# One core, a fp32 decoder trunk: the low parts of the weights at another place in a 256-byte line

## The chip, the core and the metric

The kernel runs on one core of a Trainium2 chip. The metric is the device time of one execution in microseconds (us). Before the change the median of three runs is 2539.53 us (2539.25 to 2539.55).

Five engines run side by side, each through its own queue in order: PE multiplies matrices (its weight loads, PEld, overlap its matmuls), ACT and DVE work element by element, POOL and SP here mostly start DMA transfers. SBUF is the memory on the core, 128 partitions wide; PSUM takes the sums of the matmuls. A matmul has a *stationary* operand, which a weight load brings into the array first, and a *moving* one, whose columns then stream through it.

## The reference

Two layers at sequence length 256 and width 2048, fp32 in and out: a Mamba-2 layer and an attention layer, each followed by a gated MLP with a short convolution (inner width 5632), each with a residual LayerNorm.

```python
def conv_ffn(x, w_up, conv_w, conv_b, w_down):
    u = causal_dwconv(x @ w_up, conv_w, conv_b)
    gate, val = u[..., :D_FF], u[..., D_FF:]
    return (jax.nn.silu(gate) * val) @ w_down
...
    for layer in range(DEPTH):
        if layer < N_A_LAYERS:
            mix = mamba2_mixer(h, mamba_w_in[layer], mamba_conv_w[layer], mamba_conv_b[layer],
                               mamba_dt_bias[layer], mamba_a_log[layer], mamba_d[layer],
                               mamba_norm_w[layer], mamba_w_out[layer])
        else:
            j = layer - N_A_LAYERS
            mix = moba_cross_attention(h, attn_w_q[j], attn_w_o[j], k_blk, v_blk, k_mean)
        h = layer_norm(DEEPNORM_ALPHA * h + mix, ln_mix_g[layer], ln_mix_b[layer])
        ffn = conv_ffn(h, ffn_w_up[layer], ffn_conv_w[layer], ffn_conv_b[layer], ffn_w_down[layer])
        h = layer_norm(DEEPNORM_ALPHA * h + ffn, ln_ffn_g[layer], ln_ffn_b[layer])
        if layer == N_A_LAYERS - 1:
            k_blk, v_blk, k_mean = shared_kv(h, w_kv)
```

Nearly all of the work is the products with weights: `mamba_w_in`, `mamba_w_out`, `ffn_w_up`, `ffn_w_down`, `w_kv`, `attn_w_q` and `attn_w_o`.

## The kernel before

Each fp32 number is split into a high part, rounded to float32r, and a low part, the rest. A product is the sum of three: high x high, high x low and low x high.

The weights come in 880 tiles of 512 KB (128 partitions x 1024 elements), one per *step*. `load` (L171 to L179) brings a tile into `raw` (4 buffers); `split` (L181 to L202) makes `hi` from it on ScalarE (L200) and `lo` on VectorE (L201), into four buffers each of the pool `wts`. For the few steps in `spare` the two go into free parts of the activations' buffer `hT` instead. Loads, splits and matmuls are issued in an order written out by hand: `products` (L299) issues a step's matmuls, with the splits of later steps in their midst; `at`, `beyond` and the like hang all other work on steps.

There are two ways to multiply.

- Mode "W" (the first products of a layer, for example `ffn_w_up`): the weights are stationary, 128 columns at a time, and the activations move. `some` (L241) issues, for a step, eight matmuls with `hi` stationary (L256) past which the activation's high and low parts stream together (512 columns), and eight with `lo` stationary (L259) past which the high part streams alone (256 columns). `whole` (L273) orders them in runs of one kind: 16 of `hi`, then 16 of `lo`, or 32 and 32 where two steps are paired.
- Mode "X" (the products back, for example `ffn_w_down`): the activations are stationary and the weights move, 512 columns at a time; `half` (L212) issues L222 (`hi` past the activation's high part), L223 (`lo` past the same) and L227 (`hi` past the low part). In the last steps of a chunk the pieces are 256 columns.

One small chunk (mode "H", L270) has both parts stationary.

**Places.** Call a tile's start address modulo 256 bytes its place in a line. `LINE` is 64 elements, 256 bytes. Before, all that a product with weights reads has one and the same place: `hi`, `lo`, `raw`, the activations `hT`, `yT`, `gT` and `aT`, and, as slices are 512, 1024 or 2048 bytes apart, every slice of these that is loaded or streamed. The scratch tile `u` lies 32 bytes off that place, `sz` on it.

In the Mamba layer, a group of heads uses two more tiles of 2048 bytes: `xe` (tag "xe", written at L780, read by the matmul of L803) and `sq` (tag "sq", written at L831 and L832, read by the matmul of L838), one buffer each.

Of the kernel before, what the change touches and what calls it, by code (L numbers as in the profile page):

```python
# [19 lines left out]
F32R = mybir.dt.float32r  # L20
# [4 lines left out]
P = 128  # L25
D = 2048
S = 256
# [12 lines left out]
NC = 512  # L40
HC = NC // 2
NEG = -1.0e30
LINE = 64
# [16 lines left out]
def chunks():  # L60

    z, b, c, dt = 0, 2 * DI, 2 * DI + NG * DS, 2 * DI + 2 * NG * DS

    def some(mode, name, layer, c0, n, nk):
        return [(mode, name, layer, c0 + i * NC, nk, False) for i in range(n)]

    def ffn(layer):
        up = [some(m, "ffn_w_up", layer, c + j * NC, 1, KD)[0] for j in range(DFF // NC)
              for m, c in (("W" if j else "X", 0), ("W", DFF))]
        return up + some("X", "ffn_w_down", layer, 0, 4, KF)  # L70

    out = some("W", "mamba_w_in", 0, b, 2, KD)
    out[0] = out[0][:5] + (True,)
    out += some("H", "mamba_w_in", 0, dt, 1, KD) + some("W", "mamba_w_in", 0, c, 2, KD)
    for g in range(NG):
        out += some("W", "mamba_w_in", 0, DI + g * NC, 1, KD) + some("W", "mamba_w_in", 0, z + g * NC, 1, KD)
    out += some("X", "mamba_w_out", 0, 0, 4, DI // P) + ffn(0)
    out += some("X", "w_kv", None, D, 1, KD) + some("W", "w_kv", None, 0, 4, KD) + some("W", "attn_w_q", 0, 0, 4, KD)
    return out + some("X", "w_kv", None, D + NC, 3, KD) + some("X", "attn_w_o", 0, 0, 4, KD) + ffn(1)
# [12 lines left out]
def yoco_kernel(ctx: ExitStack, tc: tile.TileContext, x, lmg, lmb, lfg, lfb, x_t, columns, w, out):  # L92
    nc = tc.nc
    base = ctx.enter_context(tc.tile_pool(name="base", bufs=1))
    wts = ctx.enter_context(tc.tile_pool(name="wts", bufs=LA + 1))
# [30 lines left out]
    steps, plan = [], chunks()  # L126
# [44 lines left out]
    def load():  # L171
        i = pos["load"]
        if i >= n_steps:
            return
        pos["load"] += 1
        t = wts.tile([P, 2, NC], F32, tag="raw", name="raw", bufs=RAW)
        for e in (slice(0, 1), slice(1, 2)) if i == 0 else (slice(0, 2),):
            nc.sync.dma_start(t[:, e], w[i][:, e])
        raw_t[i] = t  # L179

    def split():  # L181
        i = pos["split"]
        pos["split"] += 1
        t = raw_t.pop(i)
        if i in spare:
            h, l = (bufs["h"][:, k:k + 2].rearrange("p k a t -> p k (a t)") for k in (spare[i], spare[i] + 2))
        else:
            h = wts.tile([P, 2, NC], F32R, tag="hi", name="hi")
            l = wts.tile([P, 2, NC], F32R, tag="lo", name="lo")
        hi_t[i], lo_t[i] = h, l  # L190
        if steps[i][0].mode == "H":
            for a, w in enumerate((h, l)):
                v = t[:, a].rearrange("p (k n) -> p k n", k=8)
                w = w.rearrange("p a (k e n) -> p (a k) e n", e=2, n=NC // 8)
                nc.scalar.copy(w[:, :, 0], v)
                nc.vector.tensor_sub(w[:, :, 1], v, w[:, :, 0].bitcast(F32))
            return load()
        for e in ((0,), (1,)) if i < 2 else ((0, 1),):
            sl = slice(e[0], e[-1] + 1)
            nc.scalar.copy(h[:, sl], t[:, sl])  # L200
            nc.vector.tensor_sub(l[:, sl], t[:, sl], h[:, sl].bitcast(F32))  # L201
        load()  # L202

    def splits(i, most=2):

        for _ in range(1 if steps[i][0] in calm else most):
            j = pos["split"]
            ahead = LA + 1 + sum(i <= k < j for k in spare)
            if j < min(i + ahead, n_steps) and (j in spare or sum(k not in spare for k in hi_t) < LA + 1):
                split()  # L210
# [151 lines left out]
    bufs = {"h": base.tile([P, KD, 2, S], F32R, name="hT")}  # L362
# [179 lines left out]
    def open_pool(name):  # L542
        g = tc.tile_pool(name=name, bufs=1)
        pool[name] = (g, g.__enter__())
        return pool[name][1]
# [26 lines left out]
    calm.append(chB[0])  # L572
    put_x(0)
    split()
    put_x(2)
    split()
    for p in range(2, 8):
        amid(p - 2, put_x, 2 * p)


    mp = open_pool("mamba")
# [123 lines left out]
    G = [dict() for _ in range(NG)]  # L705
# [121 lines left out]
        nc.vector.tensor_add(sz[:, 0], sz[:, 0], sz[:, 1])  # L827

    def z_cut(g):
        G[g]["sq"] = q = mp.tile([P, 2, S], F32R, tag="sq", name="sq", bufs=1)  # L830
        nc.scalar.copy(q[:, 0], G[g]["sz"][:, 0])  # L831
        nc.vector.tensor_sub(q[:, 1], G[g]["sz"][:, 0], q[:, 0].bitcast(F32))  # L832

# [40 lines left out]
    for g in range(NG):  # L874
# [22 lines left out]
        at(s0 + 20, z_square, g)  # L897
        at(s0 + 21, z_sum, g)
        at(s0 + 22, z_cut, g)
        at(s0 + 23, z_rms, g)  # L900
        at(s0 + 24, z_log, g)
# [217 lines left out]
    for h in range(HEADS):  # L1119
        i, j = divmod(h, 4)  # L1120
# [87 lines left out]
```

## Time and profile before

| | |
|---|---|
| median of 3 runs | 2539.53 us |
| the profiled execution | 2539.57 us |
| its span, first to last instruction | 2537.3 us |
| granted clock of PE | 0.999 |
| weight tiles moved | 880, 512 KB each |

A row of a group has line, engine, operation, what it writes and reads, shapes, count, then the busy time in us, the mean duration of one in ns, and the idle time before it. A matmul's duration runs from its start to the modelled end of its pipeline, so the durations of a run overlap; a row of the timeline that merges n of them is n - 1 spacings and one duration long. The chain of waits counts for each matmul only the time until the next.

### The profile page before, as it was taken

The numbers are of one execution on the slowest core, as the hardware profiler recorded it, in microseconds if no ns is written. First come the engines' busy times: TensorE is split into PE (matmuls) and PEld (weight loads), VectorE is DVE, ScalarE is ACT, GpSimd is POOL, SyncE is SP. The second block draws the span as 40 slices with busy tenths as digits, with TensorE's granted clock in tenths as the row PEclk, the third lists the DMA queues.
The fourth block names the chain that finished last, engine by engine and source line by source line (L and its number), as shares of the span: only waits on it lengthen the run. The fifth ranks groups of instructions, "written<-read, shape, count | busy, mean of one in ns | idle before, by whom it ended". The sixth has DMA issues, their size and how long they took to land.

```text
span 2537.3 us, 36085 instructions
## 1 busy us (share of the span) xinstructions
PE 2524.6 (100%) x13983; PEld 2197.0 (87%) x13983; DVE 1657.9 (65%) x2140; ACT 1365.5 (54%) x1790; POOL 76.6 (3%) x96
## 2 busy tenths in 40 slices
PE   9999999999999999999999999999999999999998
PEld 8888888888888888888888888888888888888887
DVE  7778778755666766666445646645767676765545
ACT  6677787643465555554334445543555555554333
POOL 0000000000200000000000200000200000000001
PEclk9999999999999999999999999999999999999999
DMA  7666665666665555556676655456655555566664
GB/s 253 202 194 199 205 194 186 196 208 223 213 202 189 190 188 189 191 183 200 204 235 203 209 194 168 159 180 227 221 187 193 191 187 190 183 199 200 199 227 163
DMA packets 141739, 502.59 MB, mean 198 GB/s; under 512 B 15856, under 2 KB 16368, under 8 KB 141568
## 3 DMA queue, kind: packets, MB, share of 16 engines
q1 hardware_dynamic: 136448, 482.92, 58.2%
q0 software_dynamic: 4832, 16.85, 2.1%
q8 instruction: 109, 1.79, 0.3%
q14 instruction: 62, 0.51, 0.1%
q10 hardware_dynamic: 288, 0.52, 0.1%
HBM read 491.77 MB, written 8.45 MB: 197 GB/s over the span
## 4 chain that ended last, share of the span: by engine, by line
PE 99%; DMA 0%; DVE 0%; SPq 0%; issue 0%; ACT 0%
PE acc L256 40%; PE acc L259 21%; PE acc L222 11%; PE acc L223 11%; PE acc L227 11%; PE acc L794 1%; PE tp L396 0%; PE tp L227 0%; PE tp L223 0%; PE tp L222 0%; DMA raw<-in_w 0%; PE tp L803 0%; PE acc L777 0%; PE tp L1073 0%; PE tp L1107 0%; PE tp L1099 0%
## 5 line engine op out<-in xcount | busy, mean ns | idle before, releaser
L201 DVE TENSOR_TENSOR lo<-raw,hi 128x1024 fp32r<-128x1024 f32 (+1 forms) x869 | 1059.9, 1225 | 749.6 <-ACT hi L200 616.6
L200 ACT CAST hi<-raw 128x1024 fp32r<-128x1024 f32 (+1 forms) x869 | 908.6, 1048 | 857.8 <-PE acc L227 371.9
L256 PE MATMUL acc<-hT,hi 128*128 128x512 f32 x4480 | 1059.4, 391 | 1.1 <-ACT hi L200 1.1
L256 PEld LDWEIGHTS acc<-hT,hi 128*128 128x128 f32 x4480 | 828.4, 188 | 166.0 <-ACT hi L200 2.0
L259 PEld LDWEIGHTS acc<-hT,lo 128*128 128x128 f32 x4480 | 562.8, 191 | 15.8 <-issue 1.2
L259 PE MATMUL acc<-hT,lo 128*128 128x256 f32 x4480 | 570.6, 283 | 0.0
L223 PE MATMUL acc<-lo,gT 128*128 128x512 f32 (+1 forms) x678 | 254.5, 378 | 0.0
L222 PE MATMUL acc<-hi,gT 128*128 128x512 f32 (+1 forms) x678 | 254.1, 377 | 0.0
L227 PE MATMUL acc<-hi,gT 128*128 128x512 f32 (+1 forms) x678 | 200.7, 377 | 0.0
L222 PEld LDWEIGHTS acc<-hi,gT 128*128 128x128 f32 x678 | 127.6, 188 | 23.2
L223 PEld LDWEIGHTS acc<-lo,gT 128*128 128x128 f32 x678 | 127.6, 188 | 23.1
L227 PEld LDWEIGHTS acc<-hi,gT 128*128 128x128 f32 x678 | 124.8, 188 | 23.8
L223 PE MATMUL acc<-lo,yT 128*128 128x512 f32 (+1 forms) x270 | 98.6, 369 | 0.0
L222 PE MATMUL acc<-hi,yT 128*128 128x512 f32 (+1 forms) x270 | 98.5, 369 | 0.0
L222 PE MATMUL acc<-hi,hT 128*128 128x512 f32 x192 | 78.8, 410 | 0.0
L227 PE MATMUL acc<-hi,yT 128*128 128x512 f32 (+1 forms) x270 | 77.7, 369 | 0.0
L223 PE MATMUL acc<-lo,hT 128*128 128x512 f32 x192 | 75.4, 393 | 0.0
L599 DVE TENSOR_TENSOR u<-u,acc 128x512 f32<-128x512 f32 x108 | 73.4, 681 | 2.3 <-ACT u L598 1.4
L626 DVE SCALAR_TENSOR_TENSOR g<-u,cols,g 128x254 f32<-128x254 f32 (+1 forms) x176 | 73.3, 478 | 0.7 <-ACT g L621 0.7
L626 DVE SCALAR_TENSOR_TENSOR v<-u,cols,v 128x254 f32<-128x254 f32 (+1 forms) x176 | 73.0, 477 | 0.0
L1023 ACT CAST gT<-v 128x512 fp32r<-128x512 f32 x44 | 27.3, 621 | 84.5 <-DVE v L1022 84.5
L458 POOL TENSOR_TENSOR rs<-rs,mhalf 128x1 f32<-128x1 f32 x8 | 7.5, 932 | 2002.2 <-DVE nb L459 2002.2
(223 smaller groups left out, 1911.3 us busy)
## 6 DMA issues: line engine op xcount, KB each, us to landing
raw<-in_w SPq DMA_DIRECT2D x880, 512.0 KB, 3.6
mA<-acum_d POOLq DMA_DIRECT2D x16, 512.0 KB, 6.4
hres<-r POOLq DMA_DIRECT2D x12, 512.0 KB, 6.7
r<-hres SPq DMA_DIRECT2D x12, 512.0 KB, 4.9
eA<-acum_d POOLq DMA_DIRECT2D x16, 128.0 KB, 7.5
r<-in_x SPq DMA_DIRECT2D x4, 512.0 KB, 5.1
gb<-in_ln_mix_g SPq DMA_DIRECT2D x8, 256.0 KB, 4.8
gb<-in_ln_mix_b SPq DMA_DIRECT2D x8, 256.0 KB, 5.0
```

The lines of the kernel that those rows point to most:

```text
L200: nc.scalar.copy(h[:, sl], t[:, sl])
L201: nc.vector.tensor_sub(l[:, sl], t[:, sl], h[:, sl].bitcast(F32))
L222: nc.tensor.matmul(a, th, h[:, kk, sl], start=k == 0, stop=False)
L223: nc.tensor.matmul(a, th, l[:, kk, sl], start=False, stop=False)
L227: nc.tensor.matmul(a, ch.x.lo(k)[:, ts], h[:, kk, sl], start=False, stop=k == ch.nk - 1)
L256: nc.tensor.matmul(banks[j], w[:, kk, js], ch.x.both(k), start=begins, stop=ends, skip_group_check=True)
L259: nc.tensor.matmul(banks[j][:, :S], w[:, kk, js], ch.x.hi(k), start=begins, stop=ends, skip_group_check=True)
L458: nc.gpsimd.tensor_tensor(self.rs[:, h, :], self.rs[:, h, :], mhalf[:, 0, :], op=OP.pow)
L599: nc.vector.tensor_add(dst, dst, p[:, :, :S])
L626: nc.vector.scalar_tensor_tensor(d, u[:, i % 2, :S - k], c1(self.at_w, w[n - 1 - k] + self.ia + i), d, op0=OP.mult, op1=OP.add)
L794: nc.tensor.matmul(ps[64 * q:64 * q + 64, c, j * P:(j + 1) * P], G[g]["xdt"][:, c, h * 64:(h + 1) * 64], G[g]["A", c][:, h, :], start=True ...
L1023: nc.scalar.copy(h, v[:, sl])
```

## The change

In mode "W", `lo` starts 192 bytes (three quarters of a line) into its buffer; elsewhere it starts at 0 as before. The four buffers of `lo` are each a line longer, so all that is allocated behind them lies 1024 bytes higher, at the same place in a line as before. To have the room, `sq` takes the one buffer of `xe`, which has the same size.

```diff
             h = wts.tile([P, 2, NC], F32R, tag="hi", name="hi")
-            l = wts.tile([P, 2, NC], F32R, tag="lo", name="lo")
+
+            at = LINE * 3 // 4 if steps[i][0].mode == "W" else 0
+            l = wts.tile([P, 2 * NC + LINE], F32R, tag="lo", name="lo")[:, at:at + 2 * NC]
+            l = l.rearrange("p (a n) -> p a n", a=2)
         hi_t[i], lo_t[i] = h, l
```

```diff
     def z_cut(g):
-        G[g]["sq"] = q = mp.tile([P, 2, S], F32R, tag="sq", name="sq", bufs=1)
+        G[g]["sq"] = q = mp.tile([P, 2, S], F32R, tag="xe", name="sq", bufs=1)
```

In the built programs each engine has the same instructions before and after, in the same order; what differs is addresses.

## The prediction

> **What bounds the kernel now.** I read the page's shares first, then its chain that ended last.
>
> ```profile
> span 2537.3 us, 36085 instructions
> PE 2524.6 (100%) x13983; PEld 2197.0 (87%) x13983; DVE 1657.9 (65%) x2140; ACT 1365.5 (54%) x1790; POOL 76.6 (3%) x96
> ...
> PE 99%; DMA 0%; DVE 0%; SPq 0%; issue 0%; ACT 0%
> PE acc L256 40%; PE acc L259 21%; PE acc L222 11%; PE acc L223 11%; PE acc L227 11%; PE acc L794 1%; PE tp L396 0%; PE tp L227 0%; PE tp L223 0%; PE tp L222 0%; DMA raw<-in_w 0%; PE tp L803 0%; PE acc L777 0%; PE tp L1073 0%; PE tp L1107 0%; PE tp L1099 0%
> ```
>
> TensorE is never without work, and the chain is its own queue for 99% of the span. No other engine's saving can show; only the spacing from one matmul to the next can. So I need spacings, which no mean duration gives: matmuls overlap. The groups by form give counts and durations, the chain gives spacings (a run's length over its count).
>
> ```profile
> L256 PE MATMUL acc<-hT,hi 128*128 128x512 f32 x4480 | 1059.4, 391 | 1.1 <-ACT hi L200 1.1
> L259 PE MATMUL acc<-hT,lo 128*128 128x256 f32 x4480 | 570.6, 283 | 0.0
> L223 PE MATMUL acc<-lo,gT 128*128 128x512 f32 x602 | 234.6, 390 | 0.0
> ```
>
> ```profile
> 806.89 7.28 PE acc L256 x32
> 814.17 3.83 PE acc L259 x32
> ```
>
> A matmul of L256 (512 columns) costs 7.28/32 = 227.5 ns, one of L259 (256 columns) 3.83/32 = 119.7 ns. The difference, 107.8 ns for 256 columns, is 0.421 ns a column, so 256 columns alone take 107.8 ns and a matmul of either size pays about 12 ns more than its columns (12 to 13, by the rounding of the rows). These 12 ns are all that a change of place can win on a matmul of L259, which is where `lo` is stationary.
>
> **The change part by part.** In the built programs each engine has the same instructions in the same order with the same waits; only addresses differ. So nothing is added to a queue and no wait is moved; the sum is spacings times counts.
>
> *Stationary `lo` (L259), the one part with a price.* Its weight load now starts 192 bytes further in a line of 256 than the activations that stream past at that time. No matmul before has its operands at unlike places, so the trace holds no direct price. It does show that the spacing is no constant of the shape. The timeline at a switch from `hi` to `lo`, then in the middle of that run, and at the next switch back:
>
> ```profile
> 802.90 0.28 PE L259 MATMUL acc<-hT,lo 128*128 128x256 f32 x1
> ```
>
> ```profile
> 802.90 0.40 PE L259 MATMUL acc<-hT,lo 128*128 128x256 f32 x2
> ```
>
> ```profile
> 803.01 0.52 PE L259 MATMUL acc<-hT,lo 128*128 128x256 f32 x3
> ```
>
> ```profile
> 803.73 0.64 PE L259 MATMUL acc<-hT,lo 128*128 128x256 f32 x4
> ```
>
> ```profile
> 806.73 0.86 PE L256 MATMUL acc<-hT,hi 128*128 128x512 f32 x3
> ```
>
> The first `lo` matmul starts at 802.90 and the second at 803.01: 110 ns, and by the run of two 400 - 283 = 117 ns; I take 113. In the middle of the run it is (640 - 283)/3 = 119 ns. After the switch back, the first two spacings of `hi` are (860 - 391)/2 = 235 ns, 7 over the 227.5 of a run. The same instruction on the same bytes costs 6 to 7 ns less or 7 ns more by what ran before it, so what the load and the stream do to each other depends on how they stand to one another, and it settles at 120. The loads say so too:
>
> ```profile
> L259 PEld LDWEIGHTS acc<-hT,lo x4480: 186/192/193, 8.1 to 2281.9; 128*128 128x128 f32 x195
> ...
> L223 PEld LDWEIGHTS acc<-lo,gT x678: 187/188/192, 1166.0 to 2509.3; 128*128 128x128 f32 x170
> ```
>
> The median load in L259 takes 192 ns, beside the 512-column matmuls of L223 188: where columns run out soonest the load is drawn out by 4 ns. And where both operands are plain fp32, the 128-column records of L803 stand (1060 - 275)/7 = 112 ns apart, which is 256 column times plus about 4, not plus 12:
>
> ```profile
> 304.01 1.06 PE L803 MATMUL tp<-bc,xe 128*128 128x128 f32 x8
> ```
>
> That stream seems to read at half the pace beside a load of the same length, and pays a third of the extra. All three rows speak for two reads that get in each other's way, and a place 192 bytes off is a way to change it.
>
> Count: 4,480 matmuls of L259 in runs of 16 or 32; the last spacing of a run belongs to the next `hi` load, which leaves 4,200 to 4,340, say 4,280. Bounds for one spacing: the whole extra gone, -12 ns, or 4,280 x 12 = -51 us; the 7 ns that a disturbed `hi` pays added, 4,280 x 7 = +30 us, and I let the upper end reach 9 ns (+39 us), since rows are rounded to 10 ns. The row nearest to the case is L259's own spacing of 113, same shape and same engine state: -6.5 ns. Less the runs (4,480 in runs of 16 or 32 makes 140 to 280, say 190) whose first spacing has it already: 4,090 x 6.5 = -27 us.
>
> [...]
>
> *Moving `lo` (L222 to L227) keeps its place*, as do `hi`, the eight stationary `lo` of L270, the `spare` tiles and all activations; the pools behind lie 1,024 bytes higher, four whole lines. 0 us. Their spacing is already the steady one:
>
> ```profile
> 1237.80 0.45 PE acc L227 x2
> ```
>
> Bounds: a `hi` run's first spacings can change with what ran before it; (235 - 227.5) x some 4 spacings x 190 runs = 6 us either way.
>
> *VectorE writes `lo` at the new place.* Price taken 0, for two reasons. The same operation has been run at a place 32 bytes off the common one (`u`) and on it (`sz`):
>
> ```profile
> L201 DVE TENSOR_TENSOR lo<-raw,hi 128x1024 fp32r<-128x1024 f32 x865 | 1057.3, 1227 | 747.8 <-ACT hi L200 614.9 <-ACT v L621 68.3 <-ACT g L621 34.0
> L599 DVE TENSOR_TENSOR u<-u,acc 128x512 f32<-128x512 f32 x108 | 73.4, 681 | 2.3 <-ACT u L598 1.4
> ...
> L599 DVE TENSOR_TENSOR sz<-sz,acc 128x512 f32<-128x512 f32 x16 | 10.9, 678 | 0.0
> ```
>
> 681 against 678 ns. And VectorE has room in the stage with most of these writes; so has the DMA, which a faster stage would ask for 512 KB sooner. The stages with `lo` stationary (first row) and moving (second):
>
> ```profile
> 700.00:950.00 250.00, 250.00 (x1448) 221.67 (x1447) 171.76 (x227) 145.17 (x183) 0.00 (x0) 1.00 0.59 192
> ...
> 1160.00:1430.00 270.00, 269.94 (x1336) 228.11 (x1336) 149.92 (x159) 108.99 (x113) 15.59 (x18) 1.00 0.64 206
> ```
>
> After the times of PE, PEld, VectorE, ACT and POOL stand clock, DMA share and GB/s. VectorE is busy 172 of 250 us; with 32 x 6.5 ns off the 11.11 us of the two runs above, the stage is 1.9% faster and asks for 196 GB/s, and the other stage has 206. If that cover were gone, TensorE would wait for L201 and every step would carry the difference.
>
> *`sq` in the buffer of `xe`.* One buffer, so `sq` waits for the last read of `xe` and the next `xe` for the last read of `sq`. In three groups:
>
> ```profile
> L803 PE MATMUL tp<-bc,xe x24: 272/275/275, 304.0 to 403.5; 128*128 128x128 f32 x24
> L780 DVE TENSOR_TENSOR xe<-xdt,aux x3: 676/679/680, 343.8 to 442.5; 128x512 f32<-128x512 f32 x3
> ...
> L838 PE MATMUL tp<-sq,mean x6: 277/280/283, 320.9 to 419.7; 128*128 128x256 f32 x6
> L831 ACT CAST sq<-sz x3: 405/407/407, 317.6 to 416.3; 128x256 fp32r<-128x256 f32 x3
> ```
>
> `xe` is read from 304.0 (8 records, 1.06 us), `sq` written at 317.6 and read by 321, `xe` written again at 343.8: 12 and 22 us of slack. 0 us; if it were gone, some us in each of 8 groups.
>
> **Sum**: 2539.57 us (the profiled execution: span 2537.3 plus 2.3 around it; the median is 2539.53, so nothing to convert) - 27 = 2512.5, say 2512 us.
>
> **The rivals.**
>
> [...]
>
> *The new place settles worse (the slower side).* Load and stream fall into step by themselves, and 120 may be the good resting point that like places give; 192 bytes off, the load reads just behind the stream's place and each matmul of L259 pays what a disturbed `hi` pays. For: every run that leaves the resting point upwards, as L256's first two at 235, costs 7 ns. Against: those come back to 227.5 by themselves. Price: 3 to 9 ns on 4,280 spacings, 13 to 39 us; 2552 to 2578, middle 2561. It decides as soon as the steady spacing of L259 is over 120.
>
> *More than the half goes.* All extra of L259 vanishes and the disturbed spacings behind it: -51 and -6 us, 2483. For: L803's 4 ns of extra. Against: nothing of 256 columns in the trace is below 110. I count it to the forecast's side, as its far end.
>
> **How the numbers follow.** Forecast and its far end 0.60 (own range 2484 to 2532), no effect 0.10, worse place 0.30. A measurement of this kernel tells 0.2% (5 us, or 1.2 ns on a spacing of L259) from no change; of the forecast nearly all lies beyond it, and so does the slower rival: faster 0.60, same 0.10, slower 0.30. For 8 in 10 I leave out the last us of the best case and the upper half of the slower one: 2486 to 2562.
>
> **What would show it.** Right: runs of 32 of L259 in the chain shrink from 3.83 to about 3.63 us and L256's stay at 7.28; the median load in L259 falls to 188 or below; L222 to L227 stay at 0.23 a spacing. No effect: 3.83 again. Worse: 3.93 or more. Wrong in kind: a change in L256 or L223, a wait of TensorE for `lo` or `sq`, or VectorE's L201 off 1227 ns.

## The result and the profile after

The changed kernel takes 2534.45 us (median of 17 runs, 2533.92 to 2535.85) against 2539.55 us before (17 runs): ratio 0.998, 95% interval 0.9973 to 0.9987. It is faster by 5 us where 27 were forecast.

The page of the changed kernel, its lines that answer to those of before; three lines were added above, so L256 is now L259 and L259 is L262:

```profile
span 2532.6 us, 36085 instructions
PE 2520.2 (100%) x13983; PEld 2188.8 (86%) x13983; DVE 1658.3 (65%) x2140; ACT 1365.3 (54%) x1790; POOL 76.5 (3%) x96
...
PE 99%; DVE 0%; DMA 0%; issue 0%; ACT 0%; SPq 0%
...
L204 DVE TENSOR_TENSOR lo<-raw,hi 128x1024 fp32r<-128x1024 f32 (+1 forms) x869 | 1060.0, 1225 | 744.6 <-ACT hi L203 615.2
...
L259 PE MATMUL acc<-hT,hi 128*128 128x512 f32 x4480 | 1063.7, 392 | 0.9 <-ACT hi L203 0.9
...
L262 PEld LDWEIGHTS acc<-hT,lo 128*128 128x128 f32 x4480 | 554.9, 188 | 15.7 <-issue 1.2
L262 PE MATMUL acc<-hT,lo 128*128 128x256 f32 x4480 | 562.0, 280 | 0.0
```

The path is TensorE's for 99%, as before, and VectorE writes `lo` at its new place in the same 1225 ns. L262 lost 8.6 us of busy time (570.6 before), L259 gained 4.3 (1059.4 before): a gain and something given back. The chain of waits in the stage where runs are 32 long, then in a Mamba stretch where they are 16 long:

```profile
806.45 7.30 PE acc L259 x32
813.75 3.77 PE acc L262 x32
```

```profile
331.36 3.69 PE acc L259 x16
335.04 1.89 PE acc L262 x16
```

The same Mamba stretch before:

```profile
331.31 3.65 PE acc L256 x16
334.96 1.91 PE acc L259 x16
```

And the stage where the weights move, after:

```profile
1237.24 0.45 PE acc L230 x2
```

A run of 32 `lo` takes 3.77 us (117.8 ns a matmul) where it took 3.83, not the 3.63 that the forecast needs. A run of 32 `hi` takes 20 ns more, 7.30. The moving weights are as they were. The loads of `lo` (shortest, median and longest, in ns) have a median of 188, where it was 192:

```profile
L262 PEld LDWEIGHTS acc<-hT,lo x4480: 187/188/330, 9.5 to 2277.2; 128*128 128x128 f32 x195
```

The whole account, by adding up the times from each matmul's start to the next one's over the trace, in us:

| from, to | count | before | after |
|---|---|---|---|
| `lo` to `lo` (L262) | 4281 | 514.3 | 506.5 |
| `lo` to `hi` | 180 | 22.9 | 21.0 |
| `hi` to `hi` (L259, with the eight of the mode "H" chunk) | 4277 | 979.1 | 983.2 |
| weights moving past `yT`, `gT` or `aT`, 512 columns | 2801 | 636.8 | 636.8 |

The two rows of `lo` gain 9.7 us (1.2 of it a single stall of 1.36 us before), `hi` gives 4.1 back, a stall elsewhere adds 0.8: 4.8 us, and the span fell by 4.7. These stalls lie in the first 10 us of each execution and differ in every kernel below; without its own, `lo` gains 8.5 us.

### The profile page after: what moved, and what is told of

Read it like the earlier page. It is cut to its first block, busy times and chain, and to the rows that moved or that the text cites. A ratio compares the mean times of both kernels' runs of the same rounds, so it can differ in the third digit from the quotient of the medians.

```text
span 2532.6 us, 36085 instructions
## 1 busy us (share of the span) xinstructions
PE 2520.2 (100%) x13983; PEld 2188.8 (86%) x13983; DVE 1658.3 (65%) x2140; ACT 1365.3 (54%) x1790; POOL 76.5 (3%) x96
## 4 chain that ended last, share of the span: by engine, by line
PE 99%; DVE 0%; DMA 0%; issue 0%; ACT 0%; SPq 0%
PE acc L259 41%; PE acc L262 21%; PE acc L225 11%; PE acc L226 11%; PE acc L230 11%; PE acc L797 1%; PE tp L399 0%; PE tp L230 0%; PE tp L226 0%; PE tp L225 0%; PE tp L806 0%; PE acc L780 0%; PE tp L1076 0%; PE tp L1110 0%; PE tp L1102 0%; DMA raw<-in_w 0%
## 5 line engine op out<-in xcount | busy, mean ns | idle before, releaser
L204 DVE TENSOR_TENSOR lo<-raw,hi 128x1024 fp32r<-128x1024 f32 (+1 forms) x869 | 1060.0, 1225 | 744.6 <-ACT hi L203 615.2
L259 PE MATMUL acc<-hT,hi 128*128 128x512 f32 x4480 | 1063.7, 392 | 0.9 <-ACT hi L203 0.9
L259 PEld LDWEIGHTS acc<-hT,hi 128*128 128x128 f32 x4480 | 827.8, 188 | 169.5 <-ACT hi L203 1.3
L262 PEld LDWEIGHTS acc<-hT,lo 128*128 128x128 f32 x4480 | 554.9, 188 | 15.7 <-issue 1.2
L262 PE MATMUL acc<-hT,lo 128*128 128x256 f32 x4480 | 562.0, 280 | 0.0
```

What stands on the lines that cost most here:

```text
L259: nc.tensor.matmul(banks[j], w[:, kk, js], ch.x.both(k), start=begins, stop=ends, skip_group_check=True)
L262: nc.tensor.matmul(banks[j][:, :S], w[:, kk, js], ch.x.hi(k), start=begins, stop=ends, skip_group_check=True)
```

## The experiments

Theory: the weight load of the next matmul and the stream of the running one get in each other's way by their relative place in the line. Rivals: it is `lo`'s own place against what other engines read and write, or it is `sq`, or the later pools' new addresses. Then, as the size was off, what sets the size. In all kernels below `sq` lies in `xe`'s buffer; where both `hi` and `lo` get a longer buffer, the constant `tri` goes from the base pool to the Mamba pool to make room. Diffs are against before for sq_only and hT64, else against the changed kernel; `...` stands for changed lines that are left out.

**`sq` alone.**

```diff
-        G[g]["sq"] = q = mp.tile([P, 2, S], F32R, tag="sq", name="sq", bufs=1)
+        G[g]["sq"] = q = mp.tile([P, 2, S], F32R, tag="xe", name="sq", bufs=1)
```

> Before, with sq in xe's buffer and nothing else. If the gain comes from the place of lo against the activations: runs of 32 of L259 stay at 3.83 us, L256 at 7.28 us, time 2539.5 us. If it comes from sq in xe's buffer: 2534.5 us.

Measured: 2539.17 us beside 2538.91, one run each; by start times `lo` to `lo` 514.3 us and `hi` to `hi` 979.1, both as before. `sq` plays no part.

**Both parts 192 bytes off.**

```diff
-            h = wts.tile([P, 2, NC], F32R, tag="hi", name="hi")
+            h, l = (wts.tile([P, 2 * NC + LINE], F32R, tag=n, name=n)[:, at:at + 2 * NC].rearrange(
+                "p (a n) -> p a n", a=2) for n in ("hi", "lo"))
...
```

> hi and lo both 192 bytes off where they are stationary (tri moved to the Mamba pool for the room). Theory, load and stream interfere by their relative place: L259 at 117.7 ns as in the changed kernel, and L256 leaves its resting spacing of 226.7 ns too; if it falls by the same 2.2 ns and the settling at switches goes, 2515 to 2528 us, if like places suit 512 columns, over 2540 us. Rival, only the own place of lo counts: L256 as in the changed kernel, 2534.5 us.

**The activations moved instead.**

```diff
+    base.tile([P, LINE // 4], F32, name="pad0")
     bufs = {"h": base.tile([P, KD, 2, S], F32R, name="hT")}
+    base.tile([P, LINE * 3 // 4], F32, name="pad1")
...
```

> hi and lo where they were, the activations hT 64 bytes on, so that the weights stand 192 bytes off them in the line by another way (also in the 192 triples of L222 to L227 with hT stationary). Theory, the relative place counts: spacings of L256 and L259 as in both192, within 0.3 ns. Rival, the own place of lo counts (against what VectorE or ScalarE read and write): as before, 120.0 and 226.7 ns, 2539.5 us.

**`hi` alone 192 bytes off.**

```diff
+            h = wts.tile([P, 2 * NC + LINE], F32R, tag="hi", name="hi")[:, at:at + 2 * NC]
+            h = h.rearrange("p (a n) -> p a n", a=2)
+            l = wts.tile([P, 2, NC], F32R, tag="lo", name="lo")
...
```

> Only hi 192 bytes off where it is stationary, lo at the activations' place. Theory, the relative place of each pair counts: L259 back at 120.0 ns; L256 in the middle of a run as in both192; the settling at switches tells whether it hangs on hi and lo differing. Rival, only lo's place counts: all as before, 2539.5 us.

One run of each beside 2538.91 us: both192 2527.39, hT64 2531.49, hi192 2543.45. The chain of waits in the same stage as above, kernel after kernel; line numbers differ by a few, and the rows over 7 us are runs of `hi`, those under 4 us runs of `lo`. both192:

```profile
809.65 3.77 PE acc L260 x32
813.42 7.33 PE acc L257 x32
820.75 3.63 PE acc L260 x32
```

hT64:

```profile
811.36 3.77 PE acc L259 x32
815.13 7.33 PE acc L256 x32
822.46 3.63 PE acc L259 x32
```

hi192:

```profile
807.81 7.33 PE acc L258 x32
815.14 3.82 PE acc L261 x32
```

hT64 has both weights at the places where they were before and still shows the three numbers of both192, so the relative place counts and the own place of `lo` does not: the rival falls. So does that of the later pools: hT64 has the gain without the 1024 bytes of the change (its pads move everything behind by one line), and hi192 has the 1024 bytes while `lo` rests at 120 ns. Of its 4 us more than both192, 2.2 are in the 538 spacings with `hT` stationary (128.4 and 130.6 us in all), where the weights now move at an unlike place, and the rest is spread over stalls and small sums. hi192 separates the pairs: `lo` at the like place is back at 3.82, `hi` at the unlike one loses 50 ns a run whether or not `lo` is off. both192 came out inside its expected 2515 to 2528 us, but by luck: the settling of `hi` went, as that range supposed, yet `hi` rests 2.2 ns higher (228.9 against 226.7) and not lower, and what made the time is `lo` (498.4 us from `lo` to `lo`, 506.5 in the changed kernel).

The row that I had not looked for is the third one of both192. **Two runs of `lo`, same instructions, same places, take 3.77 and 3.63 us: 117.8 and 113.4 ns a matmul.** The forecast's number of 113 exists, as a second resting spacing. From the seventh spacing on, every run of twelve or more stays at one of them; both192 has 104 runs at 118 and 73 at 113.5, the changed kernel 176 and 1.

**Other places.** As both192, with both tiles 32, 64, 128 and 224 bytes off (one line for each kernel):

```diff
-            at = LINE * 3 // 4 if steps[i][0].mode == "W" else 0
+            at = LINE // 8 if steps[i][0].mode == "W" else 0
...
+            at = LINE // 4 if steps[i][0].mode == "W" else 0
...
+            at = LINE // 2 if steps[i][0].mode == "W" else 0
...
+            at = LINE * 7 // 8 if steps[i][0].mode == "W" else 0
```

> As both192 with hi and lo 32 bytes off. Theory, the relative place sets the spacing: L259 anywhere between 115 and 127 ns and L256 between 226 and 236 ns, each settled within a run, and different from both192; by a smooth dependence nearer to the like place (120.0 and 226.7). Rival, any unlike place does the same: 115.8 and 229 ns, 2527 us.

> As both192 with hi and lo 64 bytes off, the load ahead of the stream's place instead of behind it. Theory, the relative place sets the spacing and its sign counts: L259 slower than 117 ns or L256 off 229 ns. Rival, any unlike place does the same: 115.8 and 229 ns, 2527 us.

> As both192 with hi and lo half a line off, as far from the stream as can be. Theory, two reads of one place meet least where they are furthest apart: L259 at 116 ns or less, L256 at 227 ns or less, 2515 to 2527 us. Rival, any unlike place does the same: 115.8 and 229 ns, 2527 us.

> As both192 with hi and lo 224 bytes on, 32 bytes behind the stream's place. Theory, the relative place sets the spacing, by no smooth law (32, 64 and 128 bytes gave L259 119, 113.5 and 119 ns): any pair of values, each settled within a run. Rival, only multiples of 64 bytes differ from one another: as like places, 120.0 and 226.7 ns.

One run each, beside 2539.33 us (the first three) and 2539.06: 2559.24, 2536.82, 2557.70 and 2550.36 us. The chain, in that order:

```profile
810.37 3.79 PE acc L260 x32
814.16 7.46 PE acc L257 x32
```

```profile
812.73 3.63 PE acc L260 x32
816.36 7.46 PE acc L257 x32
```

```profile
808.46 3.79 PE acc L260 x32
812.25 7.47 PE acc L257 x32
```

```profile
805.87 3.73 PE acc L260 x32
809.61 7.47 PE acc L257 x32
```

For `hi`, with 512 columns, the like place is the best of these (7.28), 192 costs 50 ns a run and the others 180; that is why a shift of `hi` alone loses. For `lo`, with 256 columns, each of the unlike places is better than the like one in these runs, by no smooth law. At 64 bytes 165 of 177 long runs rest at 113.5 ns. My expectation for 128, that two reads meet least where they are furthest apart, was wrong, and so was the smooth dependence for 32. The rivals fall too: the unlike places do not all do the same, and 224 bytes, no multiple of 64, is not like 0.

**`lo` 64 bytes off, `hi` at the like place.**

```diff
-            at = LINE * 3 // 4 if steps[i][0].mode == "W" else 0
+            at = LINE // 4 if steps[i][0].mode == "W" else 0
```

> The change with 64 bytes in place of 192: hi at the activations' place, lo 64 bytes off. Theory, each pair of places has a resting spacing of its own and a switch costs a few spacings of settling: L259 at 113.5 ns as in both64 (-6.5 on 4,280 spacings, -28 us), L256 at 226.7 ns late in a run, and some 20 to 60 ns of settling per run of hi, 180 runs: 2508 to 2520 us. Rival, L259's 113.5 ns in both64 hangs on hi being off too: L259 at 117 to 120 ns, over 2530 us.

```profile
810.94 3.77 PE acc L262 x32
814.71 7.28 PE acc L259 x32
```

2530.06 us beside 2539.06, ratio 0.9965 (0.9951 to 0.9978), where 2508 to 2520 were expected. The theory as I had put it missed: `lo` is at 3.77 again, 168 long runs at 118 ns and 9 at 113.5. Its rival named the state of `hi`, and of the nine, seven follow other work than `hi`. What lo64 does show is the part given back: the first twelve spacings of a 32-run of `hi` cost together 25 ns more than twelve resting ones of 226.7, about as before (27), where the changed kernel pays 47. The new theory: the entry of a run of `lo` decides its resting spacing. In both64 the spacings of `hi`, from start to start, alternate 231 and 236 ns.

**The entry, nudged.** `lo` is 64 bytes off as in lo64, and `hi` is at the like place except at the end of a run of `hi`, where it takes `lo`'s place for eight matmuls, or for four (half a tile):

```diff
+            ends = ch.mode == "W" and (s % 4 == 1 if ch.paired else ch.kinds(s)[0] == 0)
+            h, l = (wts.tile([P, 2 * NC + LINE], F32R, tag=n, name=n)[:, o:o + 2 * NC].rearrange(
+                "p (a n) -> p a n", a=2) for n, o in (("hi", at if ends else 0), ("lo", at)))
...
```

```diff
+            h = wts.tile([P, 2 * NC + LINE], F32R, tag="hi", name="hi")[:, :2 * NC + 2 * at * ends]
+            h = h.rearrange("p (a n) -> p a n", a=2)[:, :, :NC]
...
```

> As lo64, and hi also 64 bytes off in the last 8 matmuls of each run of hi, so that runs of lo are entered as in both64 (tri in the Mamba pool for the room). Theory, L259 at an unlike place has two resting spacings, 113.5 and 118 ns, and the entry decides which: most runs of lo at 113.5 (lo64: 9 of 177, both64: 165 of 177), L259 -25 us against before, hi +8 x 6.6 ns in each of 180 runs, +9.5 us: 2522 to 2526 us. Rival, 113.5 ns hangs on hi being off throughout: most runs of lo stay at 118 ns, 2539 us.

> As nudge8 with the last 4 matmuls of each run of hi alone 64 bytes off. Theory, the entry decides: if four disturbed spacings do for the entry, 2517 to 2521 us; if they are too few or the wrong number, runs of lo stay at 118 ns and the time is about 2534 us. Rival as for nudge8: 118 ns.

2537.68 and 2533.31 us beside 2538.72, ratios 0.9995 (0.9987 to 1.0004) and 0.9979 (0.9970 to 0.9988). The chain of nudge8, then of nudge4:

```profile
813.85 3.77 PE acc L262 x32
817.62 7.33 PE acc L259 x32
```

```profile
811.88 3.77 PE acc L264 x32
815.65 7.30 PE acc L261 x32
```

Both stayed at 118 ns in most runs (153 and 152 of 177), which is what the rival had said. But the start times suggested why: nudge8 and nudge4 end `hi` on the low one of its two alternating spacings, both64 on the high one. In the four kernels where `lo` is entered from `hi` 64 bytes off (the next one among them), every one of the 323 long runs whose last spacing ahead (from the last `hi` to the first `lo`) is 230 or 231 ns rests at 118, and every one of the 345 with 233 to 236 ns at 113.5; ten more in each kernel follow other work. Four and eight are even, so an odd number should do.

**An odd number, and the change's own place.** nudge3 takes one block of the four to the front of its step, so that three are left at the end; nudge8_192 is nudge8 with 192 bytes.

```diff
+        if p == 0 and (s % 4 == 1 if ch.paired else first):
+            order = order[4:5] + order[:4] + order[5:]
...
```

> As nudge4, but an odd number of matmuls of hi, three, is 64 bytes off right before the run of lo (the fourth of that half tile is moved to the front of its step). Theory, at 64 bytes hi's spacings alternate 231 and 236 ns, and a run of lo that is entered after 236 rests at 113.5 ns, after 231 at 118 ns: with three the last is 236, most runs of lo at 113.5 ns, L259 -25 us against before, 2515 to 2522 us. Rival, the entry does not decide, or not by this: 118 ns in most runs as in nudge4, 2533 us or more.

> As nudge8 with 192 bytes in place of 64: the change, and the last 8 matmuls of each run of hi 192 bytes off too. There hi's spacings go round 226.5, 229, 231.5 ns, and in both192 the runs of lo entered after 231.5 rest at 113.5 ns, all others at 118. Theory: eight and the first load of lo make nine, so the last spacing is 231.5, most runs of lo at 113.5 ns, 2516 to 2524 us. Rival: 118 ns in most runs as in the changed kernel, 2536 us or more.

2520.80 us and 2518.68 us beside 2539.59, ratios 0.9927 (0.9915 to 0.9940) and 0.9922 (0.9908 to 0.9935), both within what was expected. The chain of nudge3:

```profile
808.80 3.63 PE acc L266 x32
812.44 7.32 PE acc L263 x32
```

and of nudge8_192:

```profile
809.18 3.63 PE acc L262 x32
812.81 7.30 PE acc L259 x32
```

Runs of `lo` at 113.5 ns: 159 of 177 and 130 of 177; with nudge4's four it was 25. So 113.5 ns does not hang on `hi` being off throughout, which was the rival of nudge8. At 192 bytes the rule is that of the three values: in both192, hT64 and nudge8_192 all 269 long runs entered after 231 or 232 ns of an unlike `hi` rest at 113.5, all others entered from `hi` at 118. So the phase at the entry decides: the rule was read off the first kernels and then held in two that were built on it. And nudge8_192 is faster than the kernel before by 21 us and than the changed one by 16 (each by its own comparison with before).

What was not tried: whether the period is 256 bytes (all places lie within one line). What the trace, which gives starts, cannot show: whether the load and the stream wait for each other in reading SBUF or elsewhere on their way, and which of the two waits.

## Why the prediction was right in direction and wrong in size

- *What bounds the kernel*: right. Apart from the stalls of the first 10 us, no wait, no other engine and no transfer entered; the span moved by what the spacings moved (4.7 and 4.8 us).
- *Two reads in each other's way by their places*: that the relative place of load and stream sets the spacing is right, and now shown by hT64, both192, sq_only and hi192; that they are in each other's way as reads stays an inference. Here the same fp32r matmuls cost 113.4, 117.8 or 119.7 ns by place and entry alone; where load and stream meet, no run shows.
- *The term that was mis-sized*: "The row nearest to the case is L259's own spacing of 113, same shape and same engine state: -6.5 ns." It went from 119.7 to 117.8 in a run of 32, -1.9 ns; all the spacings of `lo` together lost 8.5 us (the 9.7 above without the stall) instead of 27. The 113 of before was the first spacing after a switch, with both operands at like places, and not a resting value. At the new place 113.5 is one, but the changed kernel enters 176 of 177 long runs on the other side; that the two numbers agree is luck, as nothing here ties a first spacing at like places to a resting one at unlike places. "Same engine state" was the wrong half of that sentence: a run settles (before: 113.4, 119.2, then 120.0 ns), and the settled spacing was the thing to forecast.
- *The settling of `hi`*, bounded at 6 us either way and taken as 0: it cost 4.1 us, since the spacings after a switch take some ten matmuls to rest instead of five. This is why a gain of 8.5 ended as 5 (0.4 of it from the stalls).
- *Its signs*: the median load fell to 188 ns, which was to show that it was right, while the spacing fell by less than a third of what was forecast, so the load's duration did not tell the size. A change in L256 was to show that it was wrong in kind; 7.28 became 7.30, and in this part it was.
- *Its sums*: from start to start the resting spacings of before are 120.0 and 226.7 ns, so 256 columns are 106.7 and the extra is 13.3 on either size; the 12 came from whole runs, which hold the first spacings too. The middle of 2552 to 2578 is 2565 and not 2561. Neither changes the outcome.
- *VectorE, moving weights, `sq`*: each priced at 0, each 0 (1225 ns as before; 636.8 us as before; sq_only).
- *The rivals*: no effect, with its chance of 0.10, fell (ratio 0.9973 to 0.9987, and 3.77 us for a run of 32 where 3.83 was its sign); "the new place settles worse" is wrong for `lo`, and right for `hi` at each of the five places tried (229.1 to 233.4 ns in runs of 32, where the like place has 227.5). The far end, all of the extra gone, was reached by no place: 113.4 ns, half of it gone, is the least that any run rests at. The forecast's own range, 2484 to 2532 us, missed the time by 2 us.

## What to carry to other kernels

Where TensorE is never idle, look at the time from one matmul's start to the next one's in the middle of a run and just after a switch: a constant excess over the columns may depend on the operands' places (here half of it went for 256 columns, and none for 512), and a value that differs after a switch (here 113.4 ns first and 120.0 at rest) says that it is no constant of the shape. Then try the places of the two operands relative to each other, per shape, and judge by the settled spacing; a single spacing in a transient is no forecast. If a run can rest at two values, as here at 113.4 and 117.8 ns, try what stands ahead of it: here that decided, and the last eight matmuls of `hi` put off the like place were worth more (16 us) than the change itself (5 us).

## What the runs showed of the hardware that was not expected

- In these kernels the spacing of fp32r matmuls that each have a weight load depends on the relative place of the two operands. In runs of 32, 512 columns took 227.5 ns at the like place, 229.1 at 192 bytes off, 233.1 to 233.4 at 32, 64, 128 and 224; 256 columns 119.7 at the like place, 116.6 to 118.4 or 113.4 elsewhere.
- At 64 and at 192 bytes off, 256 columns have two resting spacings, 117.8 and 113.4 ns, and a run stays at one of them. What stands ahead of it decides: at 64 bytes three instead of four matmuls of `hi` off the like place put 159 of 177 runs at 113.4 instead of 25.
- A run of 512 columns at the like place after one of 256 takes five to ten matmuls to settle, 25 to 50 ns in all; at 192 bytes off (both192) no such settling shows in runs of 32 (7.33 us, which is 32 times 229.1, beside 228.9 at rest).
